# Experts of at most 32 rows on column quarters, a new order of experts, and rows read over GpSimd's queue

## The chip, the cores and the metric

The kernel runs on one core of a Trainium2 chip. The metric is the device time in microseconds, the median of the runs shown. A core has a matrix engine (TensorE, PE), a vector engine (VectorE, DVE), a scalar engine (ScalarE, ACT), GpSimd (POOL) and SyncE (SP), which here only issues DMAs. 16 DMA engines move data. A queue is named by the engine that issues into it: a DMA that has to wait for something holds up all that the same engine issues after it.

## The reference

A network of two layers. Each layer mixes its tokens in four ways (a short convolution, chunk gating, neighborhood attention, a latent attention), adds that to x, and then sends every token through two of 32 experts. Layer 0 treats 512 tokens and 256 context tokens, 768 in all; layer 1 only the 512. The experts are the part that the change is in (D = 1024, hidden width 512, all in float32):

```python
exp_logits = (hf @ w_exp + b_exp).reshape(n_tok, N_GROUPS, EXPERTS_PER_GROUP)
...
gates = p_grp * jax.nn.softmax(top_v, axis=-1)
expert_id = (g_sel * EXPERTS_PER_GROUP + top_i).reshape(-1)
...
def expert_block(args):
    xb, e = args
    return (jax.nn.silu(xb @ w_gate[e]) * (xb @ w_up[e])) @ w_down[e]
...
y = y_buf[dest].reshape(n_tok, TOP_K_INNER, d) * gates[..., None]
return jnp.sum(y, axis=1)
```

The result is multiplied by g2, a row that depends on the conditioning, and added to x. After layer 1 comes a last RMS norm.

## The kernel before

**Experts and rows.** `moe(l)` (line 1584) is one layer's experts. The device ranks the experts by the rows they got; the table `CAP` (line 29) reserves so many rows for each rank, so what is computed is fixed when the kernel is built: which expert has a rank is read at run time and only selects the weights. Two experts come first (e = 0, 1), then 26 in an `order` that spreads the large ones evenly among the small, then the last four (`NTL`), of 32 rows each. e counts the place in that order.

**Two ways to compute an expert.** One with more than 64 rows (`HW`) is *split*: each float32 weight becomes a high and a low part (ScalarE copies the high part, VectorE subtracts for the low one, lines 161 and 167), and each product is three products (`mm3`, lines 183 to 188): 48 for gate and up (`gate_up`, line 1418), 24 for down (`down`, line 1444). One with at most 64 rows stays in float32 on *halves*: `gate_up2` puts gate on TensorE's columns 0 to 63 and up on 64 to 127 (512 moving columns each, line 1394), `down2` the two halves of the result (line 1414). An instruction in float32 gives two records in the trace. `rows` (line 1367) turns the gathered rows of the next expert (line 1373), `hT1` turns the hidden rows (lines 1404 and 1406).

**Weights and slots.** An expert's weights are 12 pieces of 512 KB, and these are kept in slots of that size, some in pairs that lie side by side; `unit2` (line 130) takes one DMA of 1024 KB where two free slots are a pair. A slot is given back by `done_with` once the weights are split, or, on halves, when the products are issued in the program's order. After the last split eight more slots join, from the pool that held the split weights. `load` (line 1633) issues as far as free slots go, always on SyncE's queue, in the order of the list `lseq`.

**The experts' rows.** GpSimd gathers the rows of expert e + 3 while e is computed (line 1695), and scatters the results of each expert into an array `yd` in memory (line 1759). After the scatter of e = 27, `yload` (line 1796) reads them back: one tile of 128 tokens is two pieces of 512 KB, with T = 6 tiles in layer 0 and 4 in layer 1. `lseq` has the first half of the tiles behind the down weights of e = 28, the second half behind the gate and up weights of e = 30. In layer 0 two copies of g2 (`bc`, line 293) are loaded ahead of them, also on SyncE's queue. `accumulate` (line 1473) adds a tile to x on ScalarE and VectorE: one after the gate/up step of e = 30, T // 3 after the down step of e = 29, T // 3 after the gate/up step of e = 31, one after the down step of e = 30.

**The tail.** The last four experts don't go through memory: `tail_rows` (line 1466) multiplies their results with scaled gates into one tile `Yr`, and the products `tailw` (line 1788) bring its rows to the tokens by a table of ones. `tail_table` builds that table in steps at the down steps of the experts from e = 16 on (VectorE compares at line 1337, TensorE places at line 1342).

Of the kernel before, what the change touches and what calls it, by code (L numbers as in the profile page):

```python
# [8 lines left out]
F32 = mybir.dt.float32  # L9
# [8 lines left out]
D = 1024  # L18
# [45 lines left out]
HW = 64  # L64

# [26 lines left out]
class K:  # L92
# [37 lines left out]

    def unit2(self, src):

        n = src.shape[1] // 2
        i = self.free()
        p = self.slots[i][2]
        if i + 1 == len(self.slots) or p is None or p is not self.slots[i + 1][2] or self.slots[i + 1][1]:
            return [self.unit(src[:, j:j + n, :]) for j in (0, n)]
        v = [self.buf().rearrange("p (a b) -> p a b", a=n) for _ in range(2)]
        self.lastu = self.nc.sync.dma_start(p.rearrange("p (a b) -> p a b", a=2 * n), src)
        return v  # L140
# [1257 lines left out]
    def hT1(self, mp, h):  # L1398
        nc = self.nc
        W = h.shape[0]  # L1400
        pt = self.pss("hT")
        hv = h.rearrange("p (f k) -> p f k", k=4)
        for k in range(4):
            nc.tensor.transpose(pt[:, k * W:(k + 1) * W], hv[:, :, k], self.ident[0:W, 0:W])
        o = mp.tile([128, 2 * FE], F32R, tag="ey", name=self.nm("ehT"), bufs=3).bitcast(F32)[:, 0:4 * W]
        self.lasth2 = nc.vector.tensor_copy(o, pt[:, 0:4 * W])
        return o.rearrange("p (k t) -> p k t", k=4)

# [16 lines left out]
    def hidden(self, mp, pg):  # L1425
        h = mp.tile([128, FE], F32, tag="eh", name=self.nm("eh"), bufs=2)[0:pg.shape[0], :]
        self.lasta = self.nc.scalar.activation(h, pg, AF.Silu)  # L1427
        return h

    def hT(self, mp, h):  # L1430
# [10 lines left out]
        self.lasth2 = nc.vector.tensor_sub(f[1], pt[:, 0:4 * W], f[0].bitcast(F32))  # L1441
# [11 lines left out]
    def rows_out(self, mp, py, g2, few):  # L1453

        W = py[0].shape[0]
        y = mp.tile([128, D], F32, tag="ey", name=self.nm("ey"), bufs=3)[0:W, :]
        for n in range(2):
            c = slice(n * 512, (n + 1) * 512)
            if g2 is None:
                self.nc.scalar.copy(y[:, c], py[n])  # L1460
            else:
                a = 64 * n if few else 0
                self.nc.vector.tensor_mul(y[:, c], py[n], g2[a:a + W, c])
        return y
# [119 lines left out]
    def moe(self, l):  # L1584
# [31 lines left out]
        few = [w <= HW for w in cap]  # L1616

# [10 lines left out]
        for at, ts in ((("d", NE - 4), range(0, T // 2)), (("gu", NE - 2), range(T // 2, T))):  # L1628
# [71 lines left out]
        def rows(e):  # L1700
            if e < NE:
                xt[e] = self.rows(l, mp, X.pop(e), cap[e], few[e])
# [23 lines left out]
        for i, (m, e) in enumerate(seq):  # L1726
# [4 lines left out]
            turn = self.hT1 if few[max(e - 1, 0) if m != "d" else e] else self.hT  # L1731
# [5 lines left out]
            elif m in ("u", "gu"):  # L1737
                if m == "u":
                    pu = self.gate_up(xt.pop(e), Wt.pop((m, e)))
                else:  # L1740
                    g, pu = self.gate_up2(xt.pop(e), *Wt.pop((m, e)))
# [5 lines left out]
            else:  # L1747
# [4 lines left out]
                if few[e]:  # L1752
                    py = self.down2(ht.pop(e), w[0])
                    done_with(i)
                else:
                    py = self.down(ht.pop(e), w)
                if j < 0:
                    y = self.rows_out(mp, py, g2[0] if l else None, few[e])
# [194 lines left out]
```

## Time and profile before

| what | value |
|---|---|
| three runs | 1952.02, 1953.5 and 1957.93 us; median 1953.5 |
| the profiled execution | 1955.84 us, its span 1954.0 us |
| busy, of the span | PE 1778.1 us (91%), DVE 1014.2 (52%), ACT 739.6 (38%), POOL 247.3 (13%) |
| moved | 561.61 MB, mean 287 GB/s |
| queue q1, hardware | 511.21 MB, 69.7% of 16 engines' span |
| queue q0, software | 42.63 MB, 6.5% |
| granted TensorE clock, mean | 0.959 |

The expert stage of layer 0 runs from about 500 us to 1057, that of layer 1 from about 1400 to 1940. A share that is averaged over the whole span mixes these stages with the mixers between them; so the rows below go by stretches. In a row of windows the share of the DMA engines says whether the stretch is bound by the weights; TensorE's busy time beside it says how much it could still take. A wait of SyncE names what its next DMA waited for.

### The profile page before, as it was taken

To read this page: it belongs to the slowest core of one execution; us is meant where nothing else is said; L and a number is where in the kernel's file an instruction comes from. 1 tells how busy PE (TensorE), PEld (TensorE's weight loads), DVE (VectorE), ACT (ScalarE), POOL (GpSimd) and SP (SyncE) were. 2 spreads that over 40 slices of the span, in tenths; PEclk is the share of its full clock that TensorE was granted. 3 is DMA by queue.
4 is the path that set the end of the run, shared out by engine and by line. 5 is a ranking of instruction groups with operands and counts; after the bars stand their busy time and mean duration, and the time that the engine had idled before them with its cause. 6 is when DMAs were issued, how large, how long until landed. Compare 5 with 4: busy or idle time off the path is not lost.

```text
span 1954.0 us, 28284 instructions
## 1 busy us (share of the span) xinstructions
PE 1778.1 (91%) x10520; PEld 1106.4 (57%) x10520; DVE 1014.2 (52%) x1727; ACT 739.6 (38%) x1095; POOL 247.3 (13%) x252
## 2 busy tenths in 40 slices
PE   6999999995998999999977999998699999998996
PEld 3788788774654554445423888777444444344331
DVE  4666466546653543545327665755743444444425
ACT  4443464223552443435323555632522222222211
POOL 1000200132111111111000001013121111110000
PEclk9999999997999999999989999999799999999999
DMA  8268965534899999999977216264799999998976
GB/s 310 89 207 285 326 221 179 189 129 184 310 398 375 395 394 395 386 372 383 385 310 274 82 52 186 71 223 157 238 373 390 404 403 395 403 377 333 360 270 281
DMA packets 160318, 561.61 MB, mean 287 GB/s; under 512 B 19890, under 2 KB 46578, under 8 KB 125104
## 3 DMA queue, kind: packets, MB, share of 16 engines
q1 hardware_dynamic: 137296, 511.21, 69.7%
q0 software_dynamic: 18704, 42.63, 6.5%
q10 hardware_dynamic: 4176, 5.91, 0.9%
q8 instruction: 85, 1.39, 0.3%
q14 instruction: 57, 0.47, 0.1%
HBM read 533.54 MB, written 35.52 MB: 291 GB/s over the span
## 4 chain that ended last, share of the span: by engine, by line
PE 34%; DMA 9%; issue 6%; DVE 3%; ACT 1%; POOL 1%; SPq 0%; POOLq 0%; DVEq 0%; ACTq 0%
PE halves L1394 7%; PE halves L1414 3%; PE gate_up L187 2%; PE zunits L186 2%; PE gate_up L188 2%; PE zunits L187 2%; PE zunits L188 2%; PE gate_up L186 2%; DMA u<-in_w_gate 2%; DMA h2d<-h 2%; DMA xa<-in_w_down 1%; PE down L187 1%; PE down L188 1%; DMA u<-in_w_down 1%; PE xTw L1373 1%
## 5 line engine op out<-in xcount | busy, mean ns | idle before, releaser
L167 DVE TENSOR_TENSOR lo<-u,hi 128x1024 fp32r<-128x1024 f32 (+1 forms) x116 | 139.8, 1219 | 66.6 <-ACT hi L161 63.8
L161 ACT ACTIVATE hi<-u 128x1024 fp32r<-128x1024 f32 (+1 forms) x118 | 121.6, 1044 | 112.6 <-PE zunits L187 52.5
L187 PE MATMUL gate_up<-lo,XT 128*96 128x512 f32 (+5 forms) x368 | 153.0, 416 | 9.5 <-DVE lo L167 9.4
L186 PE MATMUL gate_up<-hi,XT 128*96 128x512 f32 (+5 forms) x368 | 152.5, 414 | 6.6 <-ACT hi L161 5.9
L1427 ACT ACTIVATE eh<-halves 32x512 f32<-32x512 f32 (+5 forms) x41 | 24.2, 589 | 349.9 <-PE halves L1394 349.9
L188 PE MATMUL gate_up<-hi,XT 128*96 128x512 f32 (+5 forms) x368 | 150.9, 410 | 2.1 <-DVE XT L1381 2.1
L167 DVE TENSOR_TENSOR lo<-xb,hi 128x1024 fp32r<-128x1024 f32 x112 | 132.5, 1220 | 31.5 <-ACT hi L161 31.0
L1695 POOL DMA_INDIRECT xb<-h2d,tok x64 | 75.1, 1173 | 556.7 <-PE xTw L1373 515.1
L1394 PE MATMUL halves<-u,XT 128*32 128x512 f32 (+5 forms) x448 | 138.8, 609 | 3.8 <-DMA u<-in_w_up 2.3
L186 PE MATMUL zunits<-hT,hi 128*128 128x512 f32 (+1 forms) x384 | 139.9, 365 | 0.9 <-ACT cqs L680 0.8
L187 PE MATMUL zunits<-hT,hi 128*128 128x512 f32 (+1 forms) x384 | 135.9, 354 | 0.0
L188 PE MATMUL zunits<-hT,lo 128*128 128x512 f32 (+1 forms) x384 | 135.3, 352 | 0.0
L1394 PE MATMUL halves<-xb,XT 128*32 128x512 f32 (+5 forms) x412 | 126.7, 602 | 3.1 <-DMA xb<-in_w_gate 1.8
L161 ACT ACTIVATE hi<-xb 128x1024 fp32r<-128x1024 f32 x112 | 113.4, 1051 | 38.9 <-PE gate_up L188 32.7
L1373 PE MATMUL xTw<-cpack,xb 32*128 32x32 f32 (+11 forms) x512 | 71.9, 284 | 37.4 <-SPq L1652 9.2
L1373 PEld LDWEIGHTS xTw<-cpack,xb 32*128 32x128 f32 (+11 forms) x512 | 63.8, 201 | 73.0 <-issue 40.3
L1759 POOL DMA_INDIRECT yd<-ey,dst x56 | 61.7, 1102 | 340.5 <-ACT ey L1460 171.1
L1394 PE MATMUL halves<-xa,XT 128*32 128x512 f32 (+5 forms) x276 | 92.0, 599 | 0.0
L1378 DVE COPY XT<-xTw 128x256 f32<-128x256 f32 (+5 forms) x41 | 20.7, 504 | 135.4 <-PE halves L1394 108.0
L186 PEld LDWEIGHTS gate_up<-hi,XT 128*96 128x96 f32 (+5 forms) x368 | 60.6, 165 | 43.8 <-ACT hi L161 12.3
L187 PEld LDWEIGHTS gate_up<-lo,XT 128*96 128x96 f32 (+5 forms) x368 | 60.7, 165 | 41.7 <-DVE lo L167 14.7
L187 PE MATMUL down<-lo,ehT 128*96 128x512 f32 (+5 forms) x184 | 77.2, 420 | 7.2 <-DVE lo L167 7.2
(420 smaller groups left out, 3621.9 us busy)
## 6 DMA issues: line engine op xcount, KB each, us to landing
u<-in_w_up SPq DMA_DIRECT2D x100, 512.0 KB
xb<-in_w_down SPq DMA_DIRECT2D x50, 1024.0 KB
u<-in_w_ada SPq DMA_DIRECT2D x96, 512.0 KB
xb<-in_w_up SPq DMA_DIRECT2D x43, 1024.0 KB
xa<-in_w_down SPq DMA_DIRECT2D x43, 1024.0 KB
xb<-in_w_gate SPq DMA_DIRECT2D x41, 1024.0 KB
u<-in_w_gate SPq DMA_DIRECT2D x64, 512.0 KB
xa<-in_w_gate SPq DMA_DIRECT2D x32, 1024.0 KB
```

What stands on the lines that cost most here:

```text
L161: self.nc.scalar.activation(h, v, AF.Copy)
L167: self.nc.vector.tensor_sub(o, v, h.bitcast(F32))
L186: mm(out, a[0], b[0], start=start, stop=False)
L187: mm(out, a[0], b[1], start=False, stop=False)
L188: self.lastm = mm(out, a[1], b[0], start=False, stop=stop)
L1373: nc.tensor.transpose(ps[:, k * 128:k * 128 + W], Xv[:, :, k], self.ident[0:W, 0:W])
L1378: nc.vector.tensor_copy(xt, v)
L1394: self.nc.tensor.matmul(ps[j], xt[:, k, :], w[k // n][:, k % n, :], start=(k == 0), stop=(k == 7), tile_position=(0, 64 * j))
L1414: self.lastm = self.nc.tensor.matmul(py[j], ht[:, k, :], ws[k // n][:, k % n, j * 512:(j + 1) * 512], start=(k == 0), stop=(k == 3), tile_ ...
L1427: self.lasta = self.nc.scalar.activation(h, pg, AF.Silu)
L1695: self.lastp = nc.gpsimd.indirect_dma_start(out=X[e][0:cap[e], :], out_offset=None, in_=self.h2d[l][:, :], in_offset=bass.IndirectOffsetOn ...
L1759: nc.gpsimd.indirect_dma_start(out=self.yd[l][:, :], in_=y, in_offset=None, out_offset=bass.IndirectOffsetOnAxis(ap=R["dst"][0:cap[e], ord ...
```

## The change

1. **Quarters.** Experts with at most 32 rows (`QW`) are computed by new functions: `gate_up4` puts gate on two quarters of TensorE's columns and up on the two others, 32 columns and 256 moving columns each, 32 instructions in place of 16; `hT4` turns the hidden rows with four transposes of 64 by 64 and two copies; `down4` computes four quarters of the result with 16 instructions in place of 8. `hidden`, `rows_out` and `tail_rows` work on these pieces. An expert of 24 rows has 32 turned. There are 5 such experts in layer 0 and 12 in layer 1, the last four of each among them.
2. **Order.** The 26 middle experts are three lists (split, halves, quarters) with costs 19, 13 and 8 (`COST`). A running sum `ahead` of cost less the mean picks the next: from the cheap end while it is above 0, from the dear end otherwise.
3. **Rows of the experts.** `yload` issues on GpSimd, with one DMA for a tile where its two slots are a pair, and the copies of g2 in layer 0 go on GpSimd too. In `lseq` the first half of the tiles now stands behind the gate and up weights of e = 30, the second behind the down weights of e = 29. `unit2` is written anew on `pair`.

The diff, cut to its core:

```diff
+QW = 32
+COST = (19, 13, 8)
...
+    def pair(self):
         i = self.free()
         p = self.slots[i][2]
-        if i + 1 == len(self.slots) or p is None or p is not self.slots[i + 1][2] or self.slots[i + 1][1]:
...
+        if i + 1 == len(self.slots) or p is not self.slots[i + 1][2] or self.slots[i + 1][1]:
+            p = None
+        return self.buf(), self.buf(), p
...
+    def gate_up4(self, xt, wg, wu):
+        ps = self.pss("quarters")[:, 0:256]
+        for k in range(8):
+            for j, w in enumerate((wg, wu)):
+                n = w[0].shape[1]
+                for i in range(2):
+                    a = 64 * j + 32 * i
+                    self.nc.tensor.matmul(ps[a:a + 32, :], xt[:, k, :], w[k // n][:, k % n, 256 * i:256 * i + 256],
+                                          start=(k == 0), stop=(k == 7), tile_position=(0, a))
+        return ps[0:64, :], ps[64:128, :]
+    def hT4(self, mp, h):
...
+            nc.tensor.transpose(pt[:, k * 64:(k + 1) * 64], hv[:, :, k], self.ident[0:64, 0:64])
...
+        for i in range(2):
+            nc.vector.tensor_copy(o[64 * i:64 * i + 64], pv[:, :, i, :])
+    def down4(self, ht, ws):
...
+            for j in range(4):
+                self.lastm = self.nc.tensor.matmul(ps[32 * j:32 * j + 32, :], ht[:, k, :],
+                                                   ws[k // n][:, k % n, 256 * j:256 * j + 256], start=(k == 0),
+                                                   stop=(k == 3), tile_position=(0, 32 * j))
...
-        n, k = NE - 2 - NTL, len(many)
-        for i in range(n):
-            order.append((many if (i + 1) * k // n > i * k // n else few).pop(0))
-        order += few
+        mean = sum(COST[i] * len(x) for i, x in enumerate(todo)) / (NE - 2 - NTL)
+        ahead = COST[0] - mean
+        while any(todo):
+            i = next(i for i in ((2, 1, 0) if ahead > 0 else (0, 1, 2)) if todo[i])
+            order.append(todo[i].pop(0))
+            ahead += COST[i] - mean
+        order += last
...
-        for at, ts in ((("d", NE - 4), range(0, T // 2)), (("gu", NE - 2), range(T // 2, T))):
+        for at, ts in ((("gu", NE - 2), range(0, T // 2)), (("d", NE - 3), range(T // 2, T))):
...
-                            g2 = [self.bc(self.buf(True), l, 3, m, nc.sync) for m in range(2)]
+                            g2 = [self.bc(self.buf(True), l, 3, m) for m in range(2)]
...
-        yt = [self.buf() for k in range(2)]
-        for k in range(2):
-            self.nc.sync.dma_start(yt[k], self.yd[l].rearrange("(p k) c -> p k c", k=2)[t * 128:(t + 1) * 128, k, :])
+        *yt, p = self.pair()
+        yd = self.yd[l].rearrange("(p k) c -> p (k c)", k=2)[t * 128:(t + 1) * 128, :]
+        for a, b in ((p, yd),) if p is not None else [(yt[k], yd[:, k * D:(k + 1) * D]) for k in range(2)]:
+            self.nc.gpsimd.dma_start(a, b)
```

**Where instructions move.** SyncE's queue near the end of layer 0's experts, before: after the down weights of e = 28 (`u<-in_w_down`) the g2 rows (`modd`), then the first three tiles of the experts' rows (`yd`), then the weights of e = 30 (`TENSOR_LOAD` reads which expert that is; `ISA` stands for register work).

```order
L148 DMA u_5088<-in_w_down 128x1024
L148 ISA
L148 DMA u_5089<-in_w_down 128x1024
L293 DMA xa_0_5077<-modd_106 128x1024 x2
L1800 DMA xa_1_5078<-yd_112 128x1024 x2
L1800 DMA xa_2_5079<-yd_112 128x1024 x2
L1800 DMA xb_0_5082<-yd_112 128x1024 x2
L1652 TENSOR_LOAD row_5237
L1652 ISA x2
L139 ISA
L139 DMA xb_1_5083<-in_w_gate 128x2048
```

The same place after the change:

```order
L148 DMA u_5088<-in_w_down 128x1024
L148 ISA
L148 DMA u_5089<-in_w_down 128x1024
L1701 TENSOR_LOAD row_5237
L1701 ISA x2
L148 ISA
L148 DMA xa_0_5077<-in_w_gate 128x2048
L148 ISA
L148 DMA xa_1_5078<-in_w_up 128x2048
```

The weights of e = 30 now follow those of e = 28 directly, in the slots `xa` and `xb`, which the g2 rows and the first tiles had before.

GpSimd at that place, before: the scatters into `yd` of the last experts that go through memory, then the first store of the next stage (`xd`).

```order
L1759 DMA yd_112<-ey_8611,dst_5228 1536x1024
L1759 DMA yd_112<-ey_8747,dst_5228 1536x1024
L1759 DMA yd_112<-ey_8854,dst_5228 1536x1024
L1759 DMA yd_112<-ey_8966,dst_5228 1536x1024
L390 DMA xd<-xres_4380 128x1024 x4
```

After:

```order
L1810 DMA yd_112<-ey_8881,dst_5228 1536x1024
L302 DMA xb_1_5083<-modd_106 128x1024 x2
L1810 DMA yd_112<-ey_9022,dst_5228 1536x1024
L1852 DMA u_8916<-yd_112 128x1024
L1852 DMA u_8917<-yd_112 128x1024
...
L1852 DMA u_8921<-yd_112 128x1024
L1852 DMA xc_0_5080<-yd_112 128x2048
L1852 DMA xc_1_5081<-yd_112 128x2048
...
L399 DMA xd<-xres_4380 128x1024 x4
```

The g2 rows stand ahead of the last scatter, the loads of the experts' rows behind it: ten in layer 0, two of them of 1024 KB, and seven in layer 1.

GpSimd near the end of layer 1's experts, before; the rows of a gather (`xb<-h2d`) tell which expert stands there: 72 is a split one, 24 and 32 are on halves.

```order
L1695 DMA xb_0_12049<-h2d_111,tok_12175 72x1024
L1759 DMA yd_113<-ey_14060,dst_12174 1024x1024
L1695 DMA xb_1_12050<-h2d_111,tok_12175 24x1024
L1759 DMA yd_113<-ey_14170,dst_12174 1024x1024
L1695 DMA xb_2_12051<-h2d_111,tok_12175 24x1024
L1759 DMA yd_113<-ey_14239,dst_12174 1024x1024
L1695 DMA xb_0_12049<-h2d_111,tok_12175 72x1024
L1759 DMA yd_113<-ey_14331,dst_12174 1024x1024
L1695 DMA xb_1_12050<-h2d_111,tok_12175 24x1024
```

After:

```order
L1744 DMA xb_1_12181<-h2d_111,tok_12306 40x1024
L1810 DMA yd_113<-ey_14853,dst_12305 1024x1024
L1744 DMA xb_0_12180<-h2d_111,tok_12306 40x1024
...
L1744 DMA xb_1_12181<-h2d_111,tok_12306 40x1024
L1810 DMA yd_113<-ey_15039,dst_12305 1024x1024
L1744 DMA xb_2_12182<-h2d_111,tok_12306 40x1024
L1810 DMA yd_113<-ey_15115,dst_12305 1024x1024
L1744 DMA xb_0_12180<-h2d_111,tok_12306 72x1024
```

Of e = 21 to 27 three were split and four on halves of 24 rows; now six are on halves of 40 rows, and one, the last, is split. In the whole layer the middle experts before were dealt out one split to two or three others; now quarters and split ones take turns from e = 2 to 16 and the halves follow.

## Rows read from the trace of the kernel before

**Rows 1.** Windows: stretch, us; busy PE, PEld, DVE, ACT, POOL; PEclk, DMA share, GB/s.

```profile
840.00:980.00 140.00, 132.91 (x608) 63.97 (x606) 60.14 (x75) 54.72 (x75) 12.54 (x13) 0.99 0.97 379
980.00:1000.00 20.00, 19.34 (x84) 7.60 (x84) 5.60 (x6) 4.52 (x7) 0.93 (x1) 1.00 0.48 161
1000.00:1040.00 40.00, 28.70 (x103) 9.12 (x104) 15.75 (x18) 5.66 (x7) 0.00 (x0) 0.83 1.02 412
1450.00:1740.00 290.00, 268.43 (x1196) 124.09 (x1193) 132.06 (x172) 77.87 (x93) 47.34 (x38) 0.97 1.02 399
1740.00:1870.00 130.00, 118.45 (x507) 51.48 (x507) 52.56 (x68) 32.32 (x41) 11.06 (x11) 0.95 0.90 345
1870.00:1890.00 20.00, 18.86 (x86) 7.54 (x84) 7.62 (x10) 5.71 (x7) 0.92 (x1) 1.00 0.32 111
1890.00:1935.00 45.00, 34.20 (x134) 8.98 (x130) 16.64 (x21) 2.94 (x5) 0.00 (x0) 0.92 0.99 396
```

**Rows 2.** SyncE: its waits (us, times, longest), then timeline (start, us) at both holes.

```profile
SPq L1800 <- DMA yd<-ey,dst: 32.0, 2, 16.3
...
974.59 0.91 SPq L293 DMA_DIRECT2D xa<-modd  x2
991.21 1.74 SPq L1800 DMA_DIRECT2D xa<-yd  x4
...
1868.67 0.33 SPq L139 DMA_DIRECT2D xb<-in_w_down  x1
1885.42 1.75 SPq L1800 DMA_DIRECT2D xb<-yd  x4
```

**Rows 3.** GpSimd: timeline of two gathers; then DMA view, KB each, us to landing.

```profile
1379.69 1.04 POOL L1695 DMA_INDIRECT xb<-h2d,tok  x1 [9.66 <-DVE nb L1263]
1381.03 0.97 POOL L1695 DMA_INDIRECT xb<-h2d,tok  x1 [0.30 <-issue]
...
bc<-modd POOLq DMA_DIRECT2D x10, 512.0 KB, 9.2
xb<-h2d,tok POOLq DMA_INDIRECT x64, 7.1
```

**Rows 4.** Chain and TensorE's timeline, 1740 to 1810: records of one expert's steps.

```profile
1741.03 0.23 PE gate_up L186
1748.51 0.99 PE xTw L1373 x8
1757.30 7.11 PE halves L1394 x30
1807.74 3.55 PE halves L1414 x16
...
1782.07 0.66 PE L1404 MATMUL hT<-cpack,eh 24*128 24x24 f32 x4
```

**Rows 5.** Timeline: the modulation product on four column tiles; weight loads of both halves.

```profile
124.15 1.93 PE L259 MATMUL ada<-u,cact 128*2 128x128 f32 x64
...
1868.89 0.11 PEld L1394 LDWEIGHTS halves<-u,XT 128*32 128x32 f32 x1 [0.31 <-issue]
1868.90 0.11 PEld L1394 LDWEIGHTS halves<-xb,XT 128*32 128x32 f32 x1
```

**Rows 6.** Timeline of TensorE: a step of the tail's table, with its wait.

```profile
1753.37 0.68 PE L1342 MATMUL tail_place<-cpack,teq 128*128 128x128 f32 x4 [2.03 <-DVE teq L1337]
```

**Rows 7.** Timeline of VectorE and TensorE at the end of both layers' experts.

```profile
1039.69 0.68 DVE L1745 TENSOR_TENSOR eh<-eh,halves 32x512 f32<-32x512 f32 x1 [1.38 <-ACT eh L1427]
1051.30 1.92 PE L1414 MATMUL halves<-u,ehT 128*32 128x512 f32 x4 [7.69 <-issue]
1057.21 10.57 PE L1788 MATMUL tailw<-u,u 128*128 128x512 f32 x24 [0.78 <-DVE u L1471]
...
1937.40 7.13 PE L1788 MATMUL tailw<-xb 128*128 128x512 f32 x16 [0.79 <-DVE xb L1471]
```

More of the change, by code (lines that the diff above doesn't have):

```diff
@@ L129, in free @@
         return next(i for i, x in enumerate(self.slots) if not x[1])
+    def pair(self):
+        i = self.free()
+        p = self.slots[i][2]
+        if i + 1 == len(self.slots) or p is not self.slots[i + 1][2] or self.slots[i + 1][1]:
+            p = None
+        return self.buf(), self.buf(), p
     def unit2(self, src):
         n = src.shape[1] // 2
-        i = self.free()
-        p = self.slots[i][2]
-        if i + 1 == len(self.slots) or p is None or p is not self.slots[i + 1][2] or self.slots[i + 1][1]:
[L137 to L140, printed above, removed]
+        a, b, p = self.pair()
+        for t, s in ((p, src),) if p is not None else ((a, src[:, :n, :]), (b, src[:, n:, :])):
+            self.lastu = self.nc.sync.dma_start(t.rearrange("p (a b) -> p a b", b=src.shape[2]), s)
+        return [t.rearrange("p (a b) -> p a b", a=n) for t in (a, b)]
     def unit(self, src, eng=None):
@@ L1451, in down, with rows_out @@
         return [p[0:W, :] for p in py]
-    def rows_out(self, mp, py, g2, few):
-        W = py[0].shape[0]
+    def rows_out(self, mp, py, g2, W):
         y = mp.tile([128, D], F32, tag="ey", name=self.nm("ey"), bufs=3)[0:W, :]
-        for n in range(2):
-            c = slice(n * 512, (n + 1) * 512)
+        n = D // len(py)
+        for i, (p, a) in enumerate(py):
+            c = slice(i * n, (i + 1) * n)
             if g2 is None:
-                self.nc.scalar.copy(y[:, c], py[n])
+                self.nc.scalar.copy(y[:, c], p[0:W, :])
             else:
-                a = 64 * n if few else 0
-                self.nc.vector.tensor_mul(y[:, c], py[n], g2[a:a + W, c])
+                self.nc.vector.tensor_mul(y[:, c], p[0:W, :], g2[a:a + W, c])
         return y
@@ L1468, in tail_rows @@
         a = slice(32 * j, 32 * j + 32)
-        for n in range(2):
-            c = slice(n * 512, (n + 1) * 512)
-            self.lastv = self.nc.vector.tensor_mul(Yr[a, c], py[n], Gs[a, c])
+        for n, (p, _) in enumerate(py):
+            c = slice(n * 256, (n + 1) * 256)
+            self.lastv = self.nc.vector.tensor_mul(Yr[a, c], p, Gs[a, c])
     def accumulate(self, l, t, yt, g, g2):
@@ L1701, in rows @@
             if e < NE:
-                xt[e] = self.rows(l, mp, X.pop(e), cap[e], few[e])
+                xt[e] = self.rows(l, mp, X.pop(e), QW if tiny[e] else cap[e], few[e])
                 gather(e + 3)
@@ L1740, in moe @@
                 else:
-                    g, pu = self.gate_up2(xt.pop(e), *Wt.pop((m, e)))
+                    g, pu = (self.gate_up4 if tiny[e] else self.gate_up2)(xt.pop(e), *Wt.pop((m, e)))
                     h[e] = self.hidden(mp, g)
@@ L1752, in moe @@
                 if few[e]:
-                    py = self.down2(ht.pop(e), w[0])
+                    py = (self.down4 if tiny[e] else self.down2)(ht.pop(e), w[0])
                     done_with(i)
@@ L1756, in moe @@
                     py = self.down(ht.pop(e), w)
+                py = [(x, n * 128 // len(py) if few[e] else 0) for n, x in enumerate(py)]
                 if j < 0:
-                    y = self.rows_out(mp, py, g2[0] if l else None, few[e])
+                    y = self.rows_out(mp, py, g2[0] if l else None, cap[e])
                     nc.gpsimd.indirect_dma_start(
```

24 lines of the change are left out of this document (20 added, 4 removed).

## The prediction

> **What bounds the kernel now.** I read the windows of the two expert stages first, because the change is inside them, then the waits of SyncE, then the chain and the prices of single products.
>
> In the steady part of layer 1's expert stage the 16 DMA engines are busy 1.02 of the time at 399 GB/s, while TensorE has 268.43 us of work in 290 [rows 1]. An expert's weights are 3 x 1024 x 512 x 4 bytes = 6.29 MB, so the stage runs at 6.29 MB / 399 GB/s = 15.8 us an expert, and less TensorE work there is worth nothing by itself. The share leaves 1.0 in two kinds of places, and only they can be won.
>
> First, a hole near the end of each layer: shares of 0.48 and 0.32 in two stretches of 20 us, and behind them TensorE has 28.70 us of work in 40 and 34.20 in 45, waiting for the weights that were not fetched [rows 1]. SyncE's waits give the cause: on the loads of the rows that the experts gave (L1800) it stands 32.0 us in two waits, the longest 16.3, for the scatters of these rows. It issues the g2 rows at 974.59 and the first of those loads at 991.21; in layer 1 a weight load at 1868.67 and the next thing at 1885.42 [rows 2]. The weights of experts 30 and 31 stand behind it in the same queue.
>
> Second, a shallow dip ahead of the hole: 0.97 for 140 us in layer 0 and 0.90 for 130 us in layer 1, with TensorE at 132.91 of 140 and 118.45 of 130 [rows 1]: there TensorE does not give weight slots back in time.
>
> **The change part by part.** The profiled run took 1955.84 us with a span of 1954.0, 2.3 us above the median of 1953.5. The sum is made against the former and taken from the median.
>
> *The loads of y and of the g2 rows leave SyncE's queue (A).* What the holes lose is (1.01 - 0.48) / 1.01 x 20 = 10.5 us in layer 0 and (1.02 - 0.32) / 1.02 x 20 = 13.7 in layer 1, 24.2 in all. TensorE's idle time behind the holes says nearly the same: 40 - 28.70 = 11.3 and 45 - 34.20 = 10.8, so 22.1 [rows 1]. The loads of expert 30 do not become free at once: their eight slots are those of expert 28's gate and up weights and of 27's down weights, given back by the products on them, so some hole stays. I take 22. From below, the one thing that surely goes is SyncE's own issue: 1.74 us for four loads [rows 2], 0.435 each, so 22 loads (20 of y, 2 of g2) are 9.6. Bounds 9.6 and 24.2.
> What is queued behind the waiting loads now? On GpSimd all gathers and scatters of the layer stand ahead of them, behind them only stores of the next stage. A GpSimd issue costs 0.97 to 1.04 us [rows 3]; 17 loads are some 17 us of an engine that has nothing else to do then. In layer 0 the g2 rows go in ahead of the last scatter, and the scaling of the tail's gates needs them early in expert 29; TensorE may wait for it about what a `bc` load takes to land, 9.2 us [rows 3]. I cost that at nothing, because the weights go on landing meanwhile; without that cover it is up to 9.
>
> A rule of the Trainium skill speaks against A ("DMA: Bandwidth & Descriptors", section "Issuing engines are not separate DMA queues"): transfers from all engines end on the same 16 DMA engines, and starting them from several saves only the sequencer's time. By it A would be 9.6, the lower bound. The rows above show the 16 engines half empty while one queue stands still, which that rule does not speak of.
>
> *Quarters.* A gate/up step of an expert on halves is 32 records; 30 of them took 7.11 us, so 7.6 in all; the down step is 3.55; turning the next expert's rows 0.99 and the hidden rows 0.66 [rows 4]; 12.8 in all. On quarters the gate/up step is 64 records of 256 columns and the down step 32. The nearest row is the modulation product: four column tiles too, 64 records of 128 columns in 1.93 us [rows 5]. Twice the columns makes 3.86, and 1.93 for down; so 7.4 an expert and 5.4 saved. From the other side, if a quarter's weights are loaded only when the products ahead are done, each record pays its 0.11 us load [rows 5]: 64 x 0.11 = 7.0, and nothing is gained. I take 3.86, since the loads of the two halves start 0.01 us apart [rows 5], so one tile's load does not wait for the other's.
> How much counts? There are 17 such experts, 5 in layer 0 and 12 in layer 1. Eight of layer 1's stand among experts 2 to 16, where DMA bounds: 8 x 7.4 + 7 x 18.3 = 187 us of TensorE against 15 x 15.8 = 237. The four last of each layer stand behind the hole. There 4 x 5.4 = 21 us less work is what keeps DMA the bound when the hole closes; it is in A already.
> The Trainium skill has a rule against it ("TensorE: Matmul & The Clock Gate", "Part 3: Packing small matmuls — row/col tiling"): a weight load overlaps running products only where the row groups differ, and column quarters share all rows. By it the price is the 7.0 of the bound.
>
> *Order of the experts (B).* The dips are worth (1.01 - 0.97) / 1.01 x 140 = 5.5 us in layer 0 and (1.02 - 0.90) / 1.02 x 130 = 15.3 in layer 1 [rows 1], 20.8 together. A split expert is 72 products of 0.23 us and 1.7 of turns, 18.3; one on halves 12.8 [rows 4]. In layer 1 experts 21 to 27 were three split and four on halves, 3 x 18.3 + 4 x 12.8 = 106 us; now they are one and six, 95, against 7 x 15.8 = 111 of DMA. So 11 us of slack comes where there was next to none beside the waits for the tail's table (2.03 us in one row [rows 6]), which stay. I take 10 of the 15.3. In layer 0 experts 20 to 27 are four and four before and after; I take 2 of 5.5. B = 12; bounds 0 (the waits and not the work set the dips) and 20.8.
>
> *End of a layer (C).* In layer 0 expert 31's hidden rows are ready on VectorE at 1039.69, but the products on them start at 1051.30 after 7.69 us idle, and the tail's product at 1057.21 [rows 7]: VectorE is adding y rows in between. These additions stand at the same steps after the change, and the rows come no earlier than they are needed. Only the short copy of the turned rows moves ahead of two additions. I take 2, bounds 0 and 9.
>
> *Small pieces (D).* Four products of 256 columns instead of two of 512 in scaling and turning, in the last experts on the path: 0.5 us lost.
>
> Sum: 22 + 12 + 2 - 0.5 = 35.5; 1955.84 - 35.5 = 1920.3 for the profiled run, 1953.5 - 35.5 = 1918 for the median.
>
> **The rivals.**
> *Only the issue is saved.* If the loads of expert 30 cannot start earlier for want of slots, A is 9.6: 9.6 + 12 + 2 - 0.5 = 23.1, so 1930. For it: those slots come back only with TensorE's products, and TensorE is busy 19.34 of the 20 us of layer 0's hole [rows 1]. Against it: 32.0 us of waiting are put down to the scatters, not to slots.
> *The clock falls.* In the stretch behind layer 0's hole, with TensorE at 28.70 of 40 us, the granted clock is 0.83, and 0.92 behind layer 1's [rows 1]. With fewer products TensorE waits more, and at 1.2 GHz in place of 2.4 what it has left costs up to double. That would take B and C: 22 - 0.5 = 21.5, so 1932. Against it: 0.97 in the steady part, where it waits 7% of the time.
> *Quarters no faster.* Then the last four experts keep their 21 us, and about a quarter of that lies behind the last weights: 5 us, so 1923.
> *Nothing changes* (within 0.3%): the holes fill but an equal wait for TensorE follows in the tail: 1953.
> *Slower.* The y loads wait on each other on GpSimd's queue. They start when the last scatter has landed, which is when SyncE goes on now, 991.21 and 1885.42 [rows 2]. If every piece of 512 KB lands only after the one before, at the 9.2 us of `bc` [rows 3], layer 0's twelve pieces take 110 us; with the 5.9 us from the last hidden products to the tail's, 1057.21 - 1051.30 [rows 7], that comes at 991.2 + 110 + 5.9 = 1107, 50 later than now. Layer 1's eight take 74, so the tail's product cannot start before 1885.4 + 74 = 1959, 22 later than its 1937.40 [rows 7]. A is lost, B stays: 1953.5 + 72 - 12 = 2013. It decides from 5.0 us a piece in layer 0, (1051.30 - 991.21) / 12, and 6.5 in layer 1, (1937.40 - 1885.42) / 8. Against it: two gathers are issued 1.3 us apart (1379.69 and 1381.03) while one lands in 7.1 [rows 3], so that queue does not wait for landings.
>
> **How the numbers follow.** Forecast 0.62 (its own range 1903 to 1930), only the issue saved 0.11, clock 0.09, quarters no faster 0.08, nothing 0.04, slower 0.06. What a measurement of this kernel can tell from no change is about 0.3%, 6 us. Faster is 0.62 + 0.11 + 0.09 + 0.08 = 0.90, same 0.04, slower 0.06. The range: all that the holes, the dips and C can give, 24.2 + 20.8 + 9 = 54, is 1899. A at its lower bound and half of B, 9.6 + 6 = 15.6, is 1938; all three lower bounds at once, 1944, I leave out. Between these lie the forecast and three rivals; the last two, 0.10, and the edges of the first four, about as much, are outside.
>
> **What would show each step.** A: no wait of SyncE on the loads of y, these on GpSimd, and a DMA share near 1 up to the last weights; a new wait for slots there would show the first rival. Quarters: gate/up near 3.9 us an expert and down near 1.9; near 7 shows the second rule. B: the share of the dip in layer 1 at 0.98 or more, in layer 0 little better. C: the time from the last hidden rows to the tail's product, 17.5 us before. The slower case would show in y pieces landing 5 us or more apart. The prediction is wrong at its root if TensorE, not the weights, turns out to end the last 100 us of a layer.

## The result and the profile after

| | before | after |
|---|---|---|
| median (runs) | 1955.72 us (4) | 1924.79 us (4: 1918.58 to 1927.35) |
| ratio, 95% interval | | 0.9836 [0.9801, 0.9871] |
| span of the profiled execution | 1954.0 us | 1925.1 us |
| PE busy | 1778.1 us | 1721.4 us |
| q0 / q1 moved | 42.63 / 511.21 MB | 54.16 / 499.67 MB |

The kernel became 31 us faster; 35.5 were forecast. To see where they came from, I cut each profiled execution at four rows that every kernel has: the first gather of each layer's experts on GpSimd, and the first `tailw` product of each on TensorE.

| us | ahead of layer 0's experts | experts, layer 0 | mixers of layer 1 | experts, layer 1 | end |
|---|---|---|---|---|---|
| before | 479.7 | 577.5 | 322.5 | 557.7 | 16.6 |
| after | 485.7 | 563.2 | 328.1 | 529.0 | 19.1 |

So the expert stages gave 14.3 + 28.7 = 43.0, and 14.1 were lost outside of them: 6.0 ahead of the first expert, where the code is the same (in the twelve kernels below it is 477.5 to 482.8, so this belongs to that one execution), and 5.6 + 2.5 right behind the experts, which will come back below.

Windows of the changed kernel, columns as in [rows 1]:

```profile
840.00:980.00 140.00, 131.05 (x634) 64.01 (x633) 62.49 (x77) 57.62 (x77) 12.74 (x13) 0.97 0.99 387
980.00:1000.00 20.00, 15.55 (x70) 7.06 (x69) 2.19 (x4) 1.06 (x2) 5.39 (x9) 0.76 0.78 301
1000.00:1040.00 40.00, 25.50 (x284) 11.01 (x282) 22.72 (x32) 9.99 (x12) 2.13 (x4) 0.71 1.02 410
1740.00:1870.00 130.00, 109.53 (x628) 44.41 (x626) 39.04 (x61) 19.10 (x25) 13.99 (x17) 0.96 1.01 411
1870.00:1890.00 20.00, 13.13 (x100) 3.97 (x100) 7.62 (x11) 0.38 (x1) 0.00 (x0) 0.50 0.99 386
1890.00:1926.00 36.00, 20.29 (x116) 6.61 (x112) 19.36 (x27) 7.53 (x15) 0.00 (x0) 0.69 0.40 162
```

Beside [rows 1]: layer 1's dip (0.90) and hole (0.32) are gone, 1.01 and 0.99 up to the last weights. In layer 0 the dip has 0.99 for 0.97 and the hole 0.78 for 0.48. And the granted clock is lower than before in the four stretches behind the dips, in which TensorE is now less busy: 0.76, 0.71, 0.50, 0.69.

What is left of layer 0's hole, in the timelines of SyncE, GpSimd and TensorE of the changed kernel, and SyncE's longest wait there (us, times, longest):

```profile
979.38 0.33 SPq L148 DMA_DIRECT2D xb<-in_w_up  x1
995.85 1.05 SPq L148 DMA_DIRECT2D xb<-in_w_down  x2
...
980.78 0.62 POOL L302 DMA_DIRECT2D xb<-modd  x1 [7.52 <-DVE lo L176]
995.37 3.23 POOL L1852 DMA_DIRECT2D u<-yd  x6 [8.31 <-issue]
...
990.52 2.07 PE L1367 MATMUL tail_scalew<-xb,gr 1*128 1x512 f32 x2 [4.45 <-DMA xb<-modd]
993.00 3.52 PE L1426 MATMUL quarters<-xb,XT 128*32 128x256 f32 x28
...
SPq L148 <- PE quarters L1426: 16.1, 2, 15.9
```

GpSimd issues the g2 rows only at 980.78, when the slot is free; TensorE wants them at 986 and stands 4.45 us. Then its products run at half speed (28 records in 3.52 us, where 28 took 1.89 in the row below), and SyncE stands 15.9 us for the slots that these products hold.

The price of quarters, in TensorE's timeline (its weight loads, PEld, last) and the chain of waits of the changed kernel:

```profile
1003.28 1.89 PE L1448 MATMUL quarters<-u,ehT 128*32 128x256 f32 x28
1005.71 1.93 PE L1426 MATMUL quarters<-xa,XT 128*32 128x256 f32 x32
...
1003.02 1.66 PEld L1448 LDWEIGHTS quarters<-u,ehT 128*32 128x32 f32 x28
...
972.01 3.60 PE quarters L1426 x60
```

60 records in 3.60 us make 3.84 for the 64 of a gate/up step, where 3.86 was estimated.

### The profile page after: what moved, and what is told of

It is laid out like the page before. It is cut to its first block, busy times and chain, and to the rows that moved or that the text cites. A ratio compares the mean times of both kernels' runs of the same rounds, so it can differ in the third digit from the quotient of the medians.

```text
span 1925.1 us, 29963 instructions
## 1 busy us (share of the span) xinstructions
PE 1721.4 (89%) x11336; PEld 1113.1 (58%) x11336; DVE 1019.4 (53%) x1776; ACT 741.8 (39%) x1097; POOL 260.4 (14%) x271
## 3 DMA queue, kind: packets, MB, share of 16 engines
q1 hardware_dynamic: 133840, 499.67, 68.8%
q0 software_dynamic: 21440, 54.16, 8.1%
## 4 chain that ended last, share of the span: by engine, by line
DMA 26%; PE 18%; DVE 3%; issue 2%; ACT 1%; POOL 1%; SPq 0%; DVEq 0%; ACTq 0%; POOLq 0%
DMA u<-in_w_up 6%; DMA xb<-in_w_up 4%; DMA xb<-in_w_down 3%; DMA xb<-in_w_gate 3%; DMA u<-in_w_down 2%; DMA xa<-in_w_down 2%; PE zunits L195 2%; PE zunits L196 2%; PE zunits L197 2%; DMA h2d<-h 2%; PE quarters L1426 1%; DMA xa<-in_w_up 1%; PE tailw L1839 1%; PE transP L839 1%; DMA u<-in_w_gate 1%
## 5 line engine op out<-in xcount | busy, mean ns | idle before, releaser
L176 DVE TENSOR_TENSOR lo<-u,hi 128x1024 fp32r<-128x1024 f32 (+1 forms) x100 | 121.2, 1219 | 59.5 <-ACT hi L170 56.4
L170 ACT ACTIVATE hi<-u 128x1024 fp32r<-128x1024 f32 (+1 forms) x102 | 105.6, 1044 | 106.1 <-PE zunits L196 52.3
L176 DVE TENSOR_TENSOR lo<-xb,hi 128x1024 fp32r<-128x1024 f32 x100 | 118.6, 1221 | 25.1 <-ACT hi L170 24.1
L176 DVE TENSOR_TENSOR lo<-xa,hi 128x1024 fp32r<-128x1024 f32 x86 | 101.8, 1220 | 27.2 <-ACT hi L170 26.4
L1387 DVE COPY XT<-xTw 128x256 f32<-128x256 f32 (+4 forms) x41 | 20.9, 511 | 173.5 <-PE halves L1403 105.9
L170 ACT ACTIVATE hi<-xa 128x1024 fp32r<-128x1024 f32 x86 | 87.5, 1053 | 32.0 <-DMA xa<-in_w_down 11.0
L1382 PEld LDWEIGHTS xTw<-cpack,xb 32*128 32x128 f32 (+10 forms) x512 | 64.1, 201 | 60.6 <-issue 26.7
L1382 PE MATMUL xTw<-cpack,xb 32*128 32x32 f32 (+10 forms) x512 | 72.0, 283 | 26.8 <-DVEq L1550 8.2
L1471 ACT ACTIVATE eh<-halves 56x512 f32<-56x512 f32 (+3 forms) x24 | 14.2, 591 | 207.0 <-PE halves L1403 207.0
L195 PE MATMUL down<-hi,ehT 128*96 128x512 f32 (+5 forms) x184 | 70.4, 444 | 16.1 <-ACT hi L170 16.1
```

The lines of the kernel that those rows point to most:

```text
L170: self.nc.scalar.activation(h, v, AF.Copy)
L176: self.nc.vector.tensor_sub(o, v, h.bitcast(F32))
L195: mm(out, a[0], b[0], start=start, stop=False)
L1382: nc.tensor.transpose(ps[:, k * 128:k * 128 + W], Xv[:, :, k], self.ident[0:W, 0:W])
L1387: nc.vector.tensor_copy(xt, v)
```

## The experiments

The theory of the prediction (theory 1): the parts have losses of their own and add up; SyncE's standing queue makes the holes, the order of experts the dips, quarters matter little beside these. Each ratio is to runs of the kernel before that were taken beside it. Stage times of all kernels, cut as above:

| kernel | ratio to before, 95% | experts 0 | mixers 1 | experts 1 | end |
|---|---|---|---|---|---|
| e1: rows over GpSimd alone | 0.9889 [0.9865, 0.9913] | 567.7 | 325.0 | 544.0 | 16.6 |
| e2: quarters alone | 0.9812 [0.9788, 0.9835] | 563.1 | 324.9 | 529.4 | 16.7 |
| e3: order alone | 0.9898 [0.9870, 0.9925] | 577.7 | 322.6 | 537.1 | 16.7 |
| e4: after without the rows | 0.9827 [0.9804, 0.9851] | 571.8 | 325.7 | 532.8 | 18.9 |
| e5: after without the order | 0.9783 [0.9756, 0.9809] | 558.4 | 328.8 | 529.2 | 19.0 |
| e6: after without quarters | 0.9817 [0.9790, 0.9843] | 567.8 | 326.4 | 531.1 | 16.6 |
| e7: after, g2 by SyncE | 0.9784 [0.9757, 0.9812] | 556.8 | 327.2 | 527.2 | 18.2 |
| e8: after, additions early | 0.9802 [0.9758, 0.9846] | 559.8 | 327.0 | 526.6 | 19.5 |
| e11: after, two products | 0.9714 [0.9690, 0.9739] | 551.2 | 333.2 | 522.1 | 18.7 |
| e13: e7 and e8 | 0.9783 [0.9757, 0.9809] | 562.6 | 323.6 | 527.7 | 18.4 |
| e14: e13 in the old order | 0.9790 [0.9765, 0.9816] | 562.0 | 325.4 | 529.0 | 16.6 |
| e15: e13, tail on halves | 0.9762 [0.9736, 0.9788] | 558.9 | 323.6 | 529.0 | 16.5 |

A stage time is of one execution each; equal code ahead of the experts differs by up to 8 us between executions (477.5 to 485.7), so differences of 3 us in one stage say little.

### One part alone

e1, on the kernel before (cut; `pair` comes with it):

```diff
-for at, ts in ((("d", NE - 4), range(0, T // 2)), (("gu", NE - 2), range(T // 2, T))):
+for at, ts in ((("gu", NE - 2), range(0, T // 2)), (("d", NE - 3), range(T // 2, T))):
-g2 = [self.bc(self.buf(True), l, 3, m, nc.sync) for m in range(2)]
+g2 = [self.bc(self.buf(True), l, 3, m) for m in range(2)]
-    self.nc.sync.dma_start(yt[k], ...)
+    self.nc.gpsimd.dma_start(a, b)
```

> The kernel before with part 3 alone: the experts' rows and g2 read over GpSimd's queue, their places in the list moved; halves and the old order stay. Theory 1 (the sum: SyncE's queue standing behind the scatters makes the holes): about 20 us faster than before, 0.99 of it, SyncE without a wait on the rows and the DMA share of the two 20-us stretches near 1. Theory 2 (the holes are TensorE's: without quarters the slots of expert 30 come no earlier): at most 10 us faster, a new wait for slots in the same place. Theory 3 (the GpSimd queue takes the pieces one by one): slower.

Measured: 9.8 us in layer 0 and 13.7 in layer 1, 23.5; the holes of [rows 1] had been priced at 10.5 and 13.7. Windows of e1, first over layer 0's old hole, then over layer 1's dip and its old hole (the layer starts 9.5 us earlier here), and SyncE's longest wait in layer 0 (us, times, longest):

```profile
980.00:1000.00 20.00, 16.11 (x51) 5.84 (x50) 2.57 (x4) 1.52 (x3) 5.37 (x9) 0.83 0.77 293
1714.20:1794.20 80.00, 70.47 (x303) 32.73 (x300) 34.61 (x46) 23.25 (x30) 7.60 (x8) 0.91 0.90 352
1794.20:1854.20 60.00, 56.04 (x241) 23.89 (x240) 26.80 (x33) 15.42 (x19) 4.51 (x4) 0.97 0.96 367
1860.00:1880.00 20.00, 18.86 (x86) 7.58 (x84) 7.31 (x9) 5.40 (x6) 0.93 (x1) 1.00 0.98 381
...
SPq L144 <- PE halves L1399: 21.6, 5, 16.3
```

In layer 1 the hole is filled (0.98 for 0.32) and the dip (0.90) stays, as theory 1 has it. In layer 0 the hole is closed by about half (0.77 for 0.48): SyncE doesn't wait for the scatters any more, but 16.3 us for slots that TensorE's products hold, the wait that theory 2 expected. In both layers together the 23.5 us are still more than the issue time (9.6). e1 changes the queue and the places in the list at once; no run parts the two.

e2, on the kernel before: quarters, nothing else (`tiny`, `gate_up4`, `hT4`, `down4`).

> The kernel before with part 1 alone: quarters for experts of at most 32 rows; the old order, and the experts' rows over SyncE as before. Theory 1: the holes stay, so 0 to 5 us faster; a gate/up step near 3.9 us and a down step near 1.9. Theory 2 (TensorE's work ahead of the end sets it): 10 to 20 us faster, since 5.4 us fall away for each of the last four experts and for four in layer 1's dip.

Measured: 14.4 us in layer 0 and 28.3 in layer 1, as much as all three parts together, and more than either theory expected. What theory 1 has of quarters falls here. SyncE's waits and its timeline in layer 0, and windows of e2:

```profile
SPq L1846 <- DMA yd<-ey,dst: 27.4, 2, 13.9
...
964.01 1.08 SPq L302 DMA_DIRECT2D xa<-modd  x2
978.70 1.75 SPq L1846 DMA_DIRECT2D xa<-yd  x4
...
960.00:975.00 15.00, 12.99 (x132) 7.12 (x124) 6.50 (x9) 7.11 (x12) 1.81 (x2) 1.00 0.98 397
975.00:990.00 15.00, 8.87 (x94) 4.60 (x84) 2.52 (x6) 1.40 (x2) 0.00 (x0) 0.79 0.76 264
1800.00:1840.00 40.00, 34.93 (x240) 17.91 (x240) 22.50 (x31) 13.54 (x15) 3.51 (x3) 0.91 1.01 409
1840.00:1860.00 20.00, 10.02 (x96) 4.07 (x98) 3.09 (x8) 1.40 (x2) 0.00 (x0) 0.68 0.81 312
```

SyncE still stands 27.4 us behind the scatters, 32.0 before [rows 2]. But what it had issued ahead now keeps the DMA engines at 0.98 until 975, with SyncE standing from 965.1 on, and then at 0.76 over 15 us (0.81 over 20 in layer 1), in place of 0.48 and 0.32 over 20. By the sum of the prediction these holes cost 3.7 and 4.1 us, 7.8 of the 24.2 before. And the dip is at 1.01 in the old order. That slots come back earlier because TensorE is done earlier is the explanation that fits; no run changes the slots alone.

e3, on the kernel before: the new order, `COST` and `ahead`, with `tiny` false for all.

> The kernel before with part 2 alone: the new order, all small experts on halves, rows over SyncE as before. Theory 1: 8 to 12 us faster, all of it in layer 1's dip (DMA share 0.98 or more in the 130 us ahead of the hole). Rival: without quarters the experts 2 to 16 of layer 1 cost TensorE 8 x 12.8 + 7 x 18.3 = 230 us against 237 of DMA, no slack is left there for waits, and the dip only moves to the front: within 4 us of before.

Measured: nothing in layer 0, 20.6 us in layer 1, twice what theory 1 expected and 5 more than the whole dip was priced at (15.3); where these 5 come from is not shown. Windows of e3 in layer 1:

```profile
1716.80:1796.80 80.00, 72.36 (x344) 26.09 (x342) 17.27 (x33) 4.06 (x9) 9.02 (x11) 0.98 1.02 407
1796.80:1856.80 60.00, 56.63 (x250) 22.48 (x247) 23.95 (x31) 14.90 (x18) 5.45 (x5) 1.00 0.99 407
1856.80:1916.80 60.00, 48.85 (x192) 13.96 (x190) 21.20 (x28) 4.27 (x6) 0.93 (x1) 0.91 0.83 325
```

The dip is filled (1.02 and 0.99), and 230 us of TensorE for 237 of DMA in front, which the rival doubted, was slack enough.

### One part taken back

e4 has y and g2 on SyncE again, at their old places in the list, e5 the old order, e6 halves for all, each in the changed kernel:

```diff
 # e4
-    self.nc.gpsimd.dma_start(a, b)
+    self.nc.sync.dma_start(yt[k], ...)
 # e5
-    i = next(i for i in ((2, 1, 0) if ahead > 0 else (0, 1, 2)) if todo[i])
+    order.append((many if (i + 1) * k // n > i * k // n else few).pop(0))
 # e6
-tiny = [w <= QW for w in cap]
+tiny = [False for w in cap]
```

> The changed kernel with part 3 undone: quarters and the new order, the experts' rows and g2 over SyncE at their old places. Theory 1: about 20 us slower than the changed kernel, so 10 to 12 faster than before, with SyncE's two waits of about 16 us back. Theory 2: within 10 us of the changed kernel.

> The changed kernel with part 2 undone: quarters and the rows over GpSimd, in the old order of experts. Theory 1 as predicted (the parts add): the dip of layer 1 is back, 8 to 12 us slower than the changed kernel. Theory F (a floor: each layer's expert stage has one idle time of the DMA engines to give, and any part that takes TensorE's or SyncE's lateness away draws on the same): within 4 us of the changed kernel, expert stages of 563 and 529 us again.

> The changed kernel with part 1 undone: the new order and the rows over GpSimd, all small experts on halves. Theory 1 as predicted: up to 5 us slower than the changed kernel. Theory F: layer 1 at its floor or within 5 us of it (order alone came within 8), layer 0 like the rows alone (568 us), so 4 to 10 us slower. Theory Q (quarters are what counts): 15 us slower or more.

Measured: none of the three is slower than the changed kernel (0.9836 [0.9801, 0.9871]) by its ratio; e5 may be faster, but the intervals overlap. By the expert stages of the single executions e4 is 12.4 us longer than the changed kernel, 8.6 of it in layer 0, with SyncE standing 29.7 us behind the scatters again; e6 is 6.7 longer and e5 4.6 shorter. So part 3 may still be worth something beside the others, which the whole times do not show. 23.5, 42.7 and 20.6 us alone would add to 86.8; together they gave 43.0, and rows and order without quarters (e6) 36.3 of 44.1. So they draw on one account, the quarters most, and it can be read: the DMA engines' busy time in an expert stage (width times share) hardly changes. Both stages before, then after:

```profile
479.70:1057.20 577.50, 522.58 (x2290) 271.11 (x2290) 273.52 (x307) 226.72 (x281) 64.24 (x61) 0.95 0.95 366
1379.70:1937.40 557.70, 501.34 (x2199) 228.30 (x2199) 248.75 (x313) 147.30 (x176) 72.71 (x61) 0.96 0.94 362
...
485.70:1048.90 563.20, 501.62 (x2531) 269.41 (x2531) 274.83 (x319) 226.47 (x283) 68.39 (x73) 0.93 0.97 375
1377.00:1906.00 529.00, 455.37 (x2774) 232.12 (x2774) 252.90 (x348) 149.65 (x176) 82.11 (x68) 0.91 0.98 381
```

Summed over shorter windows, with less lost to rounding, layer 1 before is 0.90 x 100 + 1.02 x 257.7 + 0.91 x 130 + 0.75 x 70 = 523.7 of 557.7 us; after: 0.89 x 100 + 1.02 x 229 + 1.01 x 130 + 0.91 x 70 = 517.6 of 529.0. Layer 0 by the same sum: 549.8 of 577.5, and 546.8 of 563.2. The DMA engines idled 28 + 34 us, and that is about what any part could take; after the change 16 + 11 are left. Of the 43.0 us, 35 are idle time that went; the other 8 or 9 are a smaller busy time, which the rounding of the shares may explain in part and no run explains further.

### Is that the floor?

e11 leaves the product with the low part of the rows out of the split experts:

```diff
-    def mm3(self, out, a, b, start, stop):
+    def mm3(self, out, a, b, start, stop, two=False):
...
+        if two:
+            self.lastm = mm(out, a[0], b[1], start=False, stop=stop)
+            return
...
-            self.mm3(ps[0:W, :], (xt[0][:, k, :], xt[1][:, k, :]), self.row(ws, k), k == 0, k == 7)
+            self.mm3(ps[0:W, :], (xt[0][:, k, :], xt[1][:, k, :]), self.row(ws, k), k == 0, k == 7, two=True)
```

`down` is called with `two=True` as well.

> The changed kernel with one of the three products of each split expert left out (the one with the low part of the rows and of the hidden values), which takes 24 of 72 products, about 5.5 us of TensorE, from each of the 13 split experts of layer 0 and 10 of layer 1. Theory F (the DMA engines are the floor): the expert stages change by less than 3 us each. Rival (TensorE still sets the pace in places): layer 0, which has more split experts, gets shorter by 5 us or more.

Measured: 551.2 and 522.1 us, 12 and 7 shorter than after, with TensorE busy 36.9 and 35.0 us less. The theory of a floor said less than 3, so it is too strict: in the changed kernel TensorE still costs some, in layer 0 most (7 us against e5's 558.4, too). With less of it the DMA engines' busy time is 542 of the 551 us in layer 0 (0.94 x 100 + 1.01 x 300 + 0.96 x 151.2).

### What the change adds at the end of layer 0

e7 and e8, and both in e13, on the changed kernel:

```diff
 # e7
-g2 = [self.bc(self.buf(True), l, 3, m) for m in range(2)]
+g2 = [self.bc(self.buf(True), l, 3, m, nc.sync) for m in range(2)]
 # e8
-na = dict(zip((...), (1, T // 3, T // 3, 1)))
+na = dict(zip((...), (1, T - 1, 0, 0)))
```

> The changed kernel with one thing put back: the two copies of g2 in layer 0 are issued by SyncE; the experts' rows stay on GpSimd. In the changed kernel TensorE waits 4.45 us for them at 990.5, 9.7 us after their issue. If GpSimd's queue is why they land late: that wait goes, and layer 0's expert stage is 3 to 5 us shorter. If the free slot is what they wait for, or the weights land meanwhile anyway: no change of that stage, within 1.5 us.

> The changed kernel with the additions of the experts' rows moved forward: one tile after the gate/up step of e = 30, all the others after the down step of e = 29, none behind e = 31. If VectorE's additions behind the last expert set the end of layer 0's expert stage (the chain has 14 us of VectorE there): 3 to 6 us shorter in layer 0, nothing in layer 1, where the chain ends in the last weights. If the last weights set it in layer 0 too: no change.

> The changed kernel with g2 issued by SyncE and the additions moved forward, both together. If the two are separate losses at the end of layer 0: its expert stage at about 553 us, 10 shorter than in the changed kernel (6.4 and 3.4 alone). If the first has taken the room of the second: 556, as with g2 alone.

Measured: 556.8 with g2 by SyncE, 559.8 with the additions early, against 563.2. But e5, which has neither, had 558.4: the stage of the changed kernel's one execution is at the long end, and how much of the 6.4 and 3.4 is the edit's stays open. What e7 does show is that TensorE's wait at the product with g2, 4.45 us in the changed kernel, is gone, and with it what was left of the hole (0.78). TensorE's timeline and a window of e7:

```profile
979.15 1.70 PE L1426 MATMUL quarters<-xb,XT 128*32 128x256 f32 x26
980.69 1.88 PE L1426 MATMUL quarters<-xc,XT 128*32 128x256 f32 x28
982.42 1.88 PE L1448 MATMUL quarters<-u,ehT 128*32 128x256 f32 x28
984.85 1.93 PE L1426 MATMUL quarters<-xa,XT 128*32 128x256 f32 x32
988.43 1.12 PE L1367 MATMUL tail_scalew<-xb,gr 1*128 1x512 f32 x2
...
980.00:1000.00 20.00, 18.87 (x204) 8.83 (x196) 4.11 (x7) 1.90 (x3) 5.57 (x11) 0.81 1.02 412
```

The edit did more than change a queue, though. In the changed kernel the product with g2 stands in TensorE's program behind the first 4 records of a gate/up step, so the rest of that step waits with it; in e7 it stands behind that whole step, the next down step and a further gate/up step, and in the kernel before behind the step and the down step. So it is not shown that g2 landed earlier; that the product came later would do as well. Nor does the hole follow from g2 on GpSimd alone: e8 has it (0.81 over 980 to 1000), e13 does not (1.02), but e5 has g2 on GpSimd and a wait of 3.04 us for it, and 1.00.

Both together gave 562.6, neither the 553 of two separate losses nor the 556 of one, so they do not add. ScalarE's and VectorE's timelines of e13:

```profile
1014.71 1.15 ACT L1523 ACTIVATE xc<-xc,gate 128x1024 f32<-128x1024 f32 x1 [5.14 <-DMA xc<-yd]
1015.76 1.00 ACT L1369 ACTIVATE u<-tail_scalew 128x1024 f32<-128x1024 f32 x1
...
1016.80 3.44 DVE L1514 TENSOR_TENSOR u<-quarters,u 32x256 f32<-32x256 f32 x8 [12.24 <-ACT u L1369]
```

In e13 ScalarE's scaling of the y rows stands ahead of its copy of the tail's scales and waits for rows that have not landed, and VectorE stands 12.24 us. In e8 the copy comes first, at 1002.52, so it is the pair of edits and not the additions alone. The ratios tell the same: 0.9784, 0.9802 and 0.9783, nothing gained by the second.

### The order beside quarters, and the clock

e14 is e13 with the old order; e15 is e13 with the last four experts of each layer on halves (`tail_rows` takes both widths):

```diff
-tiny = [w <= QW for w in cap]
+tiny = [w <= QW and i < NE - NTL for i, w in enumerate(cap)]
```

> As e13_g2_adds, but with the old order of experts. Theory F: within 4 us of e13_g2_adds. If the new order does any good beside quarters: e13_g2_adds is the faster one.

> As e13_g2_adds, but the last four experts of each layer on halves, 5.4 us more of TensorE for each. Clock theory: TensorE is busier ahead of the last products, these run at the full clock (16 products in 6.6 us in layer 1 in place of 8 to 9), and what follows the expert stages gets 4 to 5 us shorter in all, against up to 5 us in layer 0's expert stage. If the clock does not follow from how busy TensorE was: the products take as long as with quarters, and the kernel is 3 to 8 us slower.

Measured: the order makes no difference that shows beside quarters (0.9783 and 0.9790). The `tailw` products by line (ns min/median/max, first and last start), of the changed kernel, then of e15:

```profile
L1839 PE MATMUL tailw<-u,u x24: 592/592/1222, 1048.9 to 1061.5; 128*128 128x512 f32 x24
L1839 PE MATMUL tailw<-xb x16: 592/592/1221, 1906.0 to 1915.0; 128*128 128x512 f32 x16
...
L1840 PE MATMUL tailw<-u,u x24: 592/592/697, 1039.1 to 1049.1; 128*128 128x512 f32 x24
L1840 PE MATMUL tailw<-xb x16: 592/593/697, 1891.7 to 1898.2; 128*128 128x512 f32 x16
```

And windows ahead of layer 1's tail: of the changed kernel and of e15 from 42 us ahead of it to 21, of e14 over the same stretch; then the last 5 us ahead of it, of the changed kernel and of e14:

```profile
1864.00:1885.00 21.00, 12.67 (x96) 3.55 (x96) 3.86 (x6) 0.38 (x1) 0.00 (x0) 0.50 1.00 392
...
1850.00:1870.00 20.00, 11.61 (x40) 1.75 (x36) 3.22 (x4) 0.59 (x1) 0.00 (x0) 0.84 1.02 398
...
1857.00:1878.00 21.00, 12.01 (x94) 3.56 (x96) 3.23 (x4) 0.38 (x1) 0.00 (x0) 0.50 1.01 395
...
1901.00:1906.00 5.00, 3.56 (x28) 0.61 (x24) 4.16 (x7) 0.00 (x0) 0.00 (x0) 0.50 0.07 29
...
1894.20:1899.20 5.00, 2.25 (x32) 0.47 (x24) 1.60 (x4) 0.00 (x0) 0.00 (x0) 1.00 0.07 28
```

In the changed kernel TensorE's clock right ahead of layer 1's tail is the lower level, 1.2 GHz (0.50), and the first tail products are twice as long: 12.6 us from first to last start in layer 0 in place of the 10.0 of the kernel before, and 9.0 in place of 6.5 in layer 1. In e15 the products are as before in both layers and the rest behind the experts is back at 16.5 us; the stages cost nothing more than in e13. But e13 had layer 0's tail at full clock already (10.0), and of the 4 to 5 us that were expected 1.9 came, all behind layer 1. It is not quarters as such: in e2 and e14, with quarters in the tail, the tail products stayed at 592 to 697 ns too, and in e1 and e6, on halves, layer 0's reached 1220. Nor does the clock some 20 us earlier tell: e14 has 0.50 there like the changed kernel, and 1.00 when its tail starts. What decides it, these runs do not show. e15 is 0.9762 [0.9736, 0.9788] of before, beyond the interval of the changed kernel, 0.9836 [0.9801, 0.9871], and the lowest ratio of those that compute everything. It differs from the changed kernel in three edits, though; for the clock alone it is compared with e13 (0.9783), and there the intervals overlap.

## Why the prediction was right, and where its steps were not

The time was in the range and near the number (1918 forecast, 1924.79). What the sum had wrong is what quarters do, how far layer 0's hole closes, and what the change costs behind the experts; that these nearly cancel is luck.

**A, the queue (22 of 24.2 us).** Alone it gave 23.5 (e1). In layer 1 that is the mechanism named. In layer 0 the sign of the first rival came with it: a wait of 16.3 us for slots in e1, 15.9 in the changed kernel, and a hole closed by half; the prediction had expected some of this wait and left 2.2 us of hole in both layers for it, where e1 has about 4.8 in layer 0 alone. As a total the first rival (issue time only, 9.6) is out. The rule of the Trainium skill that was set beside it ("DMA: Bandwidth & Descriptors", "Issuing engines are not separate DMA queues") gives that 9.6, with 23.5 measured: it speaks of what starting a transfer costs, and not of a queue that stands. But the step took the hole to be the queue's alone. The hole is the queue's wait less what had been issued ahead of it: e2 leaves about 8 of the 24.2 us with the queue as it was.

**Quarters (counted at nothing of their own).** The price was right, 3.84 measured for 3.86, and the loads of the four tiles do overlap: 28 of them in 1.66 us, at 0.11 each. The rule of the Trainium skill ("TensorE: Matmul & The Clock Gate", "Part 3: Packing small matmuls — row/col tiling"), that a load overlaps running products only where the row groups differ, does not hold here, with 3.84 us against the 7.0 of the prediction's bound. What failed is the sentence on how much counts. It looked where these experts stand in the new order, among experts 2 to 16. In the old order four of layer 1's stand in the dip, 4 x 5.4 = 21.6 us of TensorE, and quarters alone fill it (1.01 in e2): 42.7 us in the two stages, where nothing had been counted. On top of the other two parts, which is what the sum asks, they add little: 6.7 us in the stages (e6 against the changed kernel), and nothing that the whole times show.

**B, the order (12).** Alone, layer 1's dip went entirely, 20.6 us where 10 were taken; layer 0 gave none, where 2 were taken. Beside quarters the order is worth nothing that these runs show (e5, e14).

**The sum.** A and B are idle time of different stretches, and these nearly add: e6, which has both and no quarters, gained 36.3 us in the stages, where A + B + C are 36. Quarters fill the same idle time over again, so the three parts together gave 43.0, 7 more than the sum. The 8.1 lost behind the stages, at which the sum had nothing, took that back.

**C (2).** In the timelines of the changed kernel:

```profile
1033.31 0.42 DVE L1795 TENSOR_TENSOR eh<-eh,quarters 64x256 f32<-64x256 f32 x1 [8.85 <-ACT eh L1471]
...
1048.87 2.08 PE L1839 MATMUL tailw<-u,u 128*128 128x512 f32 x2 [6.36 <-DVE u L1514]
```

From the last hidden rows to the tail are 15.6 us, 17.5 before: 2 gained, as forecast, but two executions can differ by as much. VectorE is still what the tail waits for there (6.36 us).

**The cost put at nothing, up to 9.** The g2 rows on GpSimd's queue cost a wait of 4.45 us and products at half the clock behind it; of layer 0's stage up to 6.4 us by e7, of which the edit's own share is open. The cover named, weights landing meanwhile, was thin: SyncE was waiting 15.9 us for slots that these products held, at a DMA share of 0.78.

**The clock.** This rival (0.09) came in part: not all of B and C, but 5.1 us in the tails themselves (2.6 + 2.5, above). That is in the 8.1 us lost behind the expert stages; the other 3.0 lie in the mixers of layer 1, which take 322.5 to 325.7 us in the kernels whose first tail ran at full clock, so they may be nothing.

**Slower.** The y pieces do not wait on each other: six were issued in 3.23 us (above), 0.54 each and not the 1 us taken from the gathers, and the longest landing of any DMA on `yd` was 21.8 us, where six pieces one after the other, at the 5.0 us from which that rival decides, would take 30.

## What to carry to other kernels

Several losses that stand in different rows can be one: where a stage has a floor or nearly one (here the weights' time on the DMA engines), first sum the idle time of that engine over the stage, and let no set of terms exceed it. Price a speed-up where its work stands in the old order as well as in the new. When a load moves to another queue, look at where the work that needs it now stands in the other engines' programs. And when an engine becomes faster than what feeds it, look at what runs right behind it: its clock may be the lower one by then.

## What was not expected of the hardware

Four column tiles with 32 columns and 256 moving columns took 32 records in 1.93 us, where 32 loads of 0.11 us one after the other would be 3.5. The clock 42 to 21 us ahead of layer 1's tail was 0.50 in the changed kernel (TensorE 12.67 us busy in 21) and in e14 (12.01), and one tail ran at the lower level and the other at the full one. GpSimd's loads of y landed late, 13.5 us for 512 KB where the `bc` rows took 9.2 before [rows 3], but many at once.
